# Attention stages of a hybrid encoder in another order on VectorE, GpSimd and TensorE

## The chip, the cores and the metric

The kernel runs on one core of one Trainium2 chip. The metric is the device time of one execution in microseconds; a kernel is measured by the median of several executions. The engines are named as the profile names them: PE is TensorE, DVE is VectorE, ACT is ScalarE, POOL is GpSimd, SP is SyncE (it issues the DMAs here).

## The reference, cut to what matters

Two requests, one of 1024 tokens and one of 512, go through the same two layers: a dilated sliding-window attention and a bidirectional S5 state-space layer. The change is in the attention layer and in the parameter tables of the S5 layer, which are computed beside it.

```python
def dilated_mixer(h, w_in, w_out):                       # 16 heads of 64
    proj = h @ w_in
    z = proj[..., 3 * N_DIL * ATTN_WIDTH:]
    for g, (window, dil) in enumerate(((128, 1), (512, 4), (2048, 16))):
        qkv = ...                                        # this group's 3 x 1024 columns of proj
        q = apply_rope(qkv[:, :, 0], cos, sin) * HEAD_DIM ** -0.5
        k = apply_rope(qkv[:, :, 1], cos, sin)
        o, lse = dilated_window_attention(q, k, qkv[:, :, 2], dil, window // (2 * dil))
    weights = jax.nn.softmax(jnp.stack(lses, axis=0), axis=0)
    o = jnp.einsum('gbsh,gbshe->bshe', weights, jnp.stack(outs, axis=0))
    return (o.reshape(bsz, s, ATTN_WIDTH) * jax.nn.silu(z)) @ w_out

def s5_mixer(h, ...):                                    # per direction
    lam_bar = jnp.exp(lam * dt)                          # its powers and products with B and C:
    b_bar = ((lam_bar - 1.0) / lam)[..., None] * b_mat   # the tables of the text below
    ...
```

## The kernel before, in words

The 1536 tokens are 12 tiles of 128. The attention works through units: a pair of heads p (8 of them) with one of the three dilation groups g. First come all (p, 0), then for each pair (p, 1), (p, 2) and a gate unit (p, 3). A unit with g below 3 has 12 steps, one per tile T; the gate unit has 3. A step is one projection of a tile into its q, k and v columns: 24 matmuls on PE (`gemm`, L885, 128x384 each; every product is made from a high and a low part, three matmuls for each of 8 slices).

**What sets the order.** The program is written by a small table of hooks. A step has 25 slots; before the matmul of slot m, whatever is hung at (step, m) is issued. All engines take their instructions in the order in which they are issued, and each waits, in that order, for what its next instruction needs. So the slots set the order on every engine and no time. A tile's further stages are hung at slots counted from the start of its own projection: one of 36 falls at slot 11 of the step after it, so that up to five tiles are in flight. The tables are `at` (L715) for the first part of a stage and `LATER` (L84) for its later parts, counted from the first.

```python
LATER = {"rope": (4, 7, 0), "qk": (3, 5, 3, 5), "soft": (5,), "et": (2, 4), "pv": (6, 6)}
at = {"rope": (0, 24), "qk": ... divmod(36, 25), "scores": divmod(max(76, ...), 25),
      "soft": divmod(79, 25), "et": divmod(100, 25), "pv": divmod(111, 25)}
```

A tile passes these stages, with the lines that the trace names:

- rope: DVE makes two products with the rotary table from the projection's result (L914, L915), POOL adds them up (L898, L899, tile t), ACT takes the values out (L941) and DVE their low part (L894).
- qk: PE transposes the rotated queries and keys into the PSUM tile qkT (L950, L951); ACT copies queries (L963) and keys (L965) out, and the keys a second time into the other half of the partitions (L971); DVE makes the low parts of the queries (L968) and of the keys (L974). Each of these is two instructions of 64x128, one for each head.
- scores: PE multiplies (L995, L999, tile sc).
- soft: DVE adds the mask and takes the row's extreme (L1022 in one form, L1025 twice), ACT makes the exponential (L1010).
- et: PE transposes the weights (L1043), ACT copies them (L1053, tile et), DVE makes their low part (L1055).
- pv: PE multiplies by the values (L1068); ACT copies the result out (L1077, L1078), POOL adds two parts onto the sum u or U (L1082).

Between them further work is hung:

- Conversion of the next unit's weights (`w_cvt`): eight per unit, ACT L842 and then L843, on DVE for even numbers and on POOL for odd ones; the first three stand at slot 16 of the unit's third, fifth and seventh step, the others in and behind its last step.
- The S5 tables: sixteen batches. A batch has 12 POOL operations of 128x512 (`prep_tab`, L1253 to L1260), two in each of six steps, and seven pairs of DVE operations (`prep_phase`, three operations for part 0, L1344 to L1346, and three for part 1, L1348 to L1350) in seven steps. Its tiles are zs and f.
- The combination of the previous pair's three groups (`combine`), in eight steps after each (p, 2), on DVE and POOL (L1169, L1179, L1178).

Of the kernel before, what the change touches and what calls it, by code (L numbers as in the profile page):

```python
# [10 lines left out]
F32 = mybir.dt.float32  # L11
# [3 lines left out]
AF = mybir.ActivationFunctionType  # L15
ALU = mybir.AluOpType
# [66 lines left out]

LATER = {"rope": (4, 7, 0), "qk": (3, 5, 3, 5), "soft": (5,), "et": (2, 4), "pv": (6, 6)}  # L84

# [55 lines left out]
class Kern:  # L141
# [550 lines left out]
    def attention(self):  # L692
        nc, I, tl = self.nc, self.I, self.tl
        H = tl.hook
# [8 lines left out]
        for u, (p, g) in enumerate(units):  # L703
            first = at_unit[p, g] = len(tl.items)
            n = NT if g < 3 else 3
            for T in range(n):
                if u == 0 and T < 2:
                    tl.idle(1)
                    i = T
                else:  # L710
                    i = tl.add(self.gemm, (p, g, T))
                if g < 3:
                    end = u + 2 == len(units)
                    early = u == 0 and T == 0
                    at = {"rope": (0, 24), "qk": (2, 2) if early else divmod(36, 25), "scores": divmod(max(76, 36 + 26 + max(LATER["qk"])), 25), "soft": divmod(79, 25), "et": divmod(100, 25), "pv": divmod(111, 25)}  # L715
                    if end:
# [9 lines left out]
                    if T == NT - 1:  # L726
                        st = divmod(25 * at["soft"][0] + at["soft"][1] + LATER["soft"][0], 25)
                        H(i + st[0], st[1], self.stats_out, p, g)
                        if g == 0:
                            H(i + at["pv"][0], at["pv"][1] + LATER["pv"][1] + 1, self.u0_store, p)  # L730
                        if end:
# [213 lines left out]
    def stage_qk(self, p, g, T, part=0):  # L945
        nc, A, B = self.nc, self.pools.get("A"), self.pools.get("B")
        if part == 0:
# [4 lines left out]
            return  # L952
        tp = self.state[(p, g, T, "tp")]
        if part == 1:
# [6 lines left out]
        if part == 1:  # L961
            for h, r, o in hs:
                nc.scalar.activation(qT[r, h], tp[r, 0:128], AF.Copy, scale=-0.125)  # L963
            for h, r, o in hs:
                nc.scalar.activation(kT[r, 0, h, c], tp[r, 128:256], AF.Copy)  # L965
        elif part == 2:
            for h, r, o in hs:
                nc.vector.scalar_tensor_tensor(qT[o, h], tp[r, 0:128], -0.125, qT[r, h].bitcast(F32), op0=ALU.mult, op1=ALU.subtract)  # L968
        elif part == 3:
            for h, r, o in hs:  # L970
                nc.scalar.activation(kT[o, 0, h, c], tp[r, 128:256], AF.Copy)  # L971
        else:
            for h, r, o in hs:
                nc.vector.tensor_tensor(kT[r, 1, h, c], tp[r, 128:256], kT[r, 0, h, c].bitcast(F32), op=ALU.subtract)  # L974
            self.state.pop((p, g, T, "tp"))

    def stage_scores(self, p, g, T):
# [255 lines left out]
    def prep_tab(self, which, part):  # L1233
# [18 lines left out]
        if part == 0:  # L1252
            g_.tensor_tensor(tr, x(xr), lr, op=ALU.mult)  # L1253
            g_.tensor_tensor(tt, x(xi), li, op=ALU.mult)
        elif part == 1:
            g_.tensor_tensor(tr, tr, tt, op=ALU.add if which == 0 else ALU.subtract)
            g_.tensor_tensor(ti, x(xi), lr, op=ALU.mult)
        else:
            g_.tensor_tensor(tt, x(xr), li, op=ALU.mult)
            g_.tensor_tensor(ti, ti, tt, op=ALU.subtract if which == 0 else ALU.add)  # L1260

# [97 lines left out]
    def prep_hooks(self, b, i):  # L1359

        H = self.tl.hook
        H(i, 0, self.prep_load, b)
        H(i + 1, 11, self.prep_cb, b)
        for k in range(3):
            H(i + 2 + k, 3, self.prep_tab, 0, k)
        H(i + 5, 11, self.prep_c_out, b)
        H(i + 5, 11, self.prep_lag, b, 0)
        H(i + 5, 16, self.prep_lag, b, 1)
        H(i + 5, 21, self.prep_lag_out, b, 0)
        H(i + 5, 21, self.prep_lag_out, b, 1)  # L1370
        for k in range(3):
            H(i + 6 + k, 7, self.prep_tab, 1, k)
        H(i + 9, 0, self.prep_b_out, b, 0)
        H(i + 9, 20, self.prep_b_out, b, 1)
        for j in range(7):
            H(i + 2 + j, 15, self.prep_phase, b, j, 0)
            H(i + 2 + j, 21, self.prep_phase, b, j, 1)

# [643 lines left out]
```

## Time and profile before

| what | value |
|---|---|
| runs (device us) | 3187.55, 3179.74, 3178.81; median 3179.74 |
| the profiled execution's own time | 3181.66 us |
| its span | 3179.8 us |
| granted clock of PE, mean | 0.975 of full speed |
| busy: PE, DVE, ACT, POOL | 2829.9 (89%), 2200.0 (69%), 1848.4 (58%), 1498.9 (47%) us |
| attention, units and hooks as above | about 57 to 2277 us of the span |

Busy time is what an engine spends in its instructions; the rest is idle time, and the trace names for each idle stretch the instruction whose end released the engine. Matmuls overlap in the engine, so a start of the next is a better mark than the end of the one before. A stretch (a window) of the span is given as start:end in us.

### The profile page before, as it was taken

To read this page: it belongs to the slowest core of one execution; us is meant where nothing else is said; L and a number is where in the kernel's file an instruction comes from. 1 tells how busy PE (TensorE), PEld (TensorE's weight loads), DVE (VectorE), ACT (ScalarE), POOL (GpSimd) and SP (SyncE) were. 2 spreads that over 40 slices of the span, in tenths; PEclk is the share of its full clock that TensorE was granted. 3 is DMA by queue.
4 is the path that set the end of the run, shared out by engine and by line. 5 is a ranking of instruction groups with operands and counts; after the bars stand their busy time and mean duration, and the time that the engine had idled before them with its cause. 6 is when DMAs were issued, how large, how long until landed. Compare 5 with 4: busy or idle time off the path is not lost.

```text
span 3179.8 us, 51898 instructions
## 1 busy us (share of the span) xinstructions
PE 2829.9 (89%) x16181; PEld 2439.5 (77%) x16181; DVE 2200.0 (69%) x6071; ACT 1848.4 (58%) x5696; POOL 1498.9 (47%) x2081
## 2 busy tenths in 40 slices
PE   6799999997788888888888888888989989889998
PEld 5788888887777878778787878778778766667887
DVE  7677777775776676757666676757664699984445
ACT  5877777777676766667576676667644222223221
POOL 3645555453653453535344453535365466552243
PEclk8999999998899999999999999999999999999999
DMA  7122232221122212221222222121354545436553
GB/s 205 51 85 76 83 81 77 71 85 48 45 82 56 62 48 57 57 66 44 60 58 55 58 51 66 42 72 52 96 163 123 170 158 176 164 121 182 166 159 126
DMA packets 428227, 293.73 MB, mean 92 GB/s; under 512 B 140288, under 2 KB 379152, under 8 KB 427824
## 3 DMA queue, kind: packets, MB, share of 16 engines
q1 hardware_dynamic: 427808, 290.16, 31.8%
q8 instruction: 128, 2.10, 0.3%
q14 instruction: 147, 1.20, 0.1%
q10 hardware_dynamic: 144, 0.26, 0.0%
HBM read 204.72 MB, written 85.62 MB: 91 GB/s over the span
## 4 chain that ended last, share of the span: by engine, by line
PE 38%; DVE 21%; ACT 15%; POOL 9%; issue 9%; DMA 7%; SPq 1%; POOLq 0%; DVEq 0%; ACTq 0%
PE mm L885 13%; PE mm L1652 8%; DMA wraw<-in_attn_w_in 3%; ACT e L1010 3%; ACT kT L971 2%; DVE et L1055 2%; DVE kT L974 2%; ACT kT L965 2%; PE sc L1845 2%; ACT pw L1077 2%; PE mm L1845 2%; PE pv L1068 2%; DVE t L914 2%; DVE qT L968 2%; ACT qT L963 2%
## 5 line engine op out<-in xcount | busy, mean ns | idle before, releaser
L885 PE MATMUL mm<-whl,hp 128*128 128x384 f32 x4584 | 967.3, 354 | 7.6 <-ACT hp L356 2.8
L885 PEld LDWEIGHTS mm<-whl,hp 128*128 128x128 f32 x4584 | 817.4, 197 | 27.5 <-issue 12.9
L885 PE MATMUL mm<-whl,hs 128*128 128x384 f32 x2304 | 486.5, 352 | 0.8 <-ACT hs L270 0.4
L1082 POOL TENSOR_TENSOR u<-u,pw 128x128 f32<-128x128 f32 x384 | 197.8, 515 | 523.7 <-ACT u L1078 508.1
L885 PEld LDWEIGHTS mm<-whl,hs 128*128 128x128 f32 x2304 | 406.3, 194 | 9.5 <-issue 7.2
L968 DVE SCALAR_TENSOR_TENSOR qT<-qkT,qT 64x128 fp32r<-64x128 f32 x576 | 166.4, 289 | 341.9 <-ACT kT L971 324.0
L1010 ACT ACTIVATE e<-e,st 128x128 f32<-128x128 f32 (+2 forms) x576 | 250.3, 435 | 152.1 <-DVE st L1025 151.7
L1652 PE MATMUL mm<-hp,wi 128*128 128x512 f32 x1104 | 280.8, 403 | 2.7 <-ACT sig L1689 2.7
L1068 PE MATMUL pv<-et,vs 128*128 128x256 f32 x704 | 159.2, 306 | 131.3 <-DVE et L1055 130.9
L1068 PEld LDWEIGHTS pv<-et,vs 128*128 128x128 f32 x704 | 115.3, 191 | 178.2 <-DVE et L1055 175.0
L1652 PEld LDWEIGHTS mm<-hp,wi 128*128 128x128 f32 x1104 | 203.9, 189 | 54.1 <-issue 8.6
L898 POOL TENSOR_TENSOR t<-t,t 128x128 f32<-128x128 f32 x288 | 137.7, 478 | 206.9 <-DVE t L915 195.0
L1077 ACT ACTIVATE pw<-pv 64x256 f32<-64x256 f32 x576 | 217.9, 378 | 9.8
L941 ACT ACTIVATE vs<-mm 64x128 fp32r<-64x128 f32 (+1 forms) x350 | 96.0, 274 | 206.8 <-DVE t L915 203.8
L1082 POOL TENSOR_TENSOR U<-U,pw 128x128 f32<-128x128 f32 x192 | 91.7, 478 | 238.4 <-ACT U L1078 230.9
L1055 DVE TENSOR_TENSOR et<-eT,et 128x512 fp32r<-128x512 f32 (+1 forms) x288 | 162.9, 566 | 34.7 <-ACT et L1053 34.3
L963 ACT ACTIVATE qT<-qkT 64x128 fp32r<-64x128 f32 x576 | 155.2, 269 | 54.3 <-PE qkT L951 48.0
L843 POOL TENSOR_TENSOR whl<-wraw,whl 128x384 fp32r<-128x384 f32 (+1 forms) x116 | 116.6, 1005 | 142.8 <-ACT whl L842 139.6
L974 DVE TENSOR_TENSOR kT<-qkT,kT 64x128 fp32r<-64x128 f32 x576 | 166.4, 289 | 9.8
L971 ACT ACTIVATE kT<-qkT 64x128 fp32r<-64x128 f32 x576 | 156.9, 272 | 8.1
L965 ACT ACTIVATE kT<-qkT 64x128 fp32r<-64x128 f32 x576 | 156.9, 272 | 6.8
L999 PE MATMUL sc<-kT,qT 128*128 128x192 f32 (+2 forms) x704 | 125.9, 291 | 39.1 <-DVE kT L974 38.3
(368 smaller groups left out, 6314.5 us busy)
## 6 DMA issues: line engine op xcount, KB each, us to landing
wraw<-in_attn_w_in SPq DMA_DIRECT2D x192, 192.0 KB
par<-par_d SPq DMA_DIRECT2D x64, 512.0 KB
f<-f_d SPq DMA_DIRECT2D x44, 384.0 KB
par_d<-zs SPq DMA_DIRECT2D x64, 256.0 KB
U<-in_ada_w SPq DMA_DIRECT2D x16, 768.0 KB
par_d<-f SPq DMA_DIRECT2D x64, 128.0 KB
raw<-in_ssm_w_in SPq DMA_DIRECT2D x14, 512.0 KB
u_d<-u SPq DMA_DIRECT2D x8, 768.0 KB
```

The source lines that it names most:

```text
L885: nc.tensor.matmul(ps[:, :384], self.hv(a, k, self.tok_cols(g, T)), self.wt[((p, g), k)][:, b], start=m == 0, stop=m == 23)
L963: nc.scalar.activation(qT[r, h], tp[r, 0:128], AF.Copy, scale=-0.125)
L965: nc.scalar.activation(kT[r, 0, h, c], tp[r, 128:256], AF.Copy)
L968: nc.vector.scalar_tensor_tensor(qT[o, h], tp[r, 0:128], -0.125, qT[r, h].bitcast(F32), op0=ALU.mult, op1=ALU.subtract)
L971: nc.scalar.activation(kT[o, 0, h, c], tp[r, 128:256], AF.Copy)
L974: nc.vector.tensor_tensor(kT[r, 1, h, c], tp[r, 128:256], kT[r, 0, h, c].bitcast(F32), op=ALU.subtract)
L1010: nc.scalar.activation(e[:, h, :W], e[:, h, :W], AF.Exp, scale=-1.0, bias=st[:, T, h, 0:1], accum_out=st[:, T, h, 1:2])
L1055: nc.vector.tensor_tensor(et[:, 1, 0:n], tp[:, 0:n], et[:, 0, 0:n].bitcast(F32), op=ALU.subtract)
L1068: nc.tensor.matmul(pv[:, h], V[key][:, 2 * h:2 * h + 2].rearrange("p a c -> p (a c)"), et[:, :, ci, h], start=ci == 0, stop=ci == len(chun ...
L1077: nc.scalar.activation(w[hi], pv[hi, h], AF.Copy)
L1082: nc.gpsimd.tensor_tensor(u, u, w[:, a], op=ALU.add)
L1652: nc.tensor.matmul(st["ps"], state[("w", u)][a][:, k], self.hv(b, k, slice(512 * c, 512 * c + 512)), start=m == 0, stop=m == 23)
```

## The change

Five edits, all in the order of issue but one:

1. The second copy of the keys (into the other half of the partitions) is made by POOL from the first copy in SBUF, not by ACT from PSUM. The first copy, the queries' and the keys' low parts are then hung together.
2. DVE's mask for one tile now comes ahead of the low part of the weights of the tile before, and the low part of the values moves to one slot later.
3. The queries' and keys' transposes move two matmuls later (36 to 38), the product with the values seven (111 to 118).
4. The tables on POOL are hung one operation at a time, at slots 8 and 19, instead of two at slot 3 or 7. The two additions of each half go over the tile as it lies (128x512 in one run) instead of through the four-dimensional view that the products need.
5. DVE's phase work moves from slots 15 and 21 to 18 and 22.

```diff
-LATER = {"rope": (4, 7, 0), "qk": (3, 5, 3, 5), "soft": (5,), "et": (2, 4), "pv": (6, 6)}
+LATER = {"rope": (4, 8, 0), "qk": (3, 5, 5), "soft": (5,), "et": (2, 6), "pv": (6, 6)}
...
-"qk": ... divmod(36, 25), "scores": divmod(max(76, 36 + 26 + max(LATER["qk"])), 25), ... "pv": divmod(111, 25)}
+"qk": ... divmod(38, 25), "scores": divmod(76, 25), ... "pv": divmod(118, 25)}
...
         elif part == 2:
             for h, r, o in hs:
                 nc.vector.scalar_tensor_tensor(qT[o, h], tp[r, 0:128], -0.125, ...)
-        elif part == 3:
-            for h, r, o in hs:
-                nc.scalar.activation(kT[o, 0, h, c], tp[r, 128:256], AF.Copy)
-        else:
             for h, r, o in hs:
                 nc.vector.tensor_tensor(kT[r, 1, h, c], tp[r, 128:256], kT[r, 0, h, c].bitcast(F32), op=ALU.subtract)
             self.state.pop((p, g, T, "tp"))
+        else:
+            for h, r, o in hs:
+                nc.gpsimd.tensor_copy(kT[o, 0, h, c], kT[r, 0, h, c].bitcast(F32))
...
-            g_.tensor_tensor(tr, tr, tt, op=ALU.add if which == 0 else ALU.subtract)
+            g_.tensor_tensor(P["tr"], P["tr"], P["tt"], op=ALU.add if which == 0 else ALU.subtract)
...
-            g_.tensor_tensor(ti, ti, tt, op=ALU.subtract if which == 0 else ALU.add)
+            g_.tensor_tensor(P["ti"], P["ti"], P["tt"], op=ALU.subtract if which == 0 else ALU.add)
...
-        for k in range(3):
-            H(i + 2 + k, 3, self.prep_tab, 0, k)
+        for k in range(6):
+            H(i + 2 + k // 2, (8, 19)[k % 2], self.prep_tab, 0, k)
...
-        for k in range(3):
-            H(i + 6 + k, 7, self.prep_tab, 1, k)
+        for k in range(6):
+            H(i + 6 + k // 2, (8, 19)[k % 2], self.prep_tab, 1, k)
...
-            H(i + 2 + j, 15, self.prep_phase, b, j, 0)
-            H(i + 2 + j, 21, self.prep_phase, b, j, 1)
+            H(i + 2 + j, 18, self.prep_phase, b, j, 0)
+            H(i + 2 + j, 22, self.prep_phase, b, j, 1)
```

**PE, one plain step.** The rows around the products with the values (pv, from the weights et and the values vs, ve) and the transposes of queries and keys (qkT). Before:

```order
L885 MATMUL mm<-whl,hp_122 128x384 x2
L1068 MATMUL pv<-et,vs 128x256
L1068 MATMUL pv<-et,ve_588 128x256
L1068 MATMUL pv<-et,vs 128x256
L1068 MATMUL pv<-et,ve_588 128x256
L950 MATMUL qkT<-ident,t_10951 128x128
L951 MATMUL qkT<-ident,t_10951 128x128
L885 MATMUL mm<-whl,hp_123 128x384
```

And with the change:

```order
L885 MATMUL mm<-whl,hp_531 128x384
L950 MATMUL qkT<-ident,t_10951 128x128
L951 MATMUL qkT<-ident,t_10951 128x128
L885 MATMUL mm<-whl,hp_531 128x384
L885 MATMUL mm<-whl,hp_532 128x384
L885 MATMUL mm<-whl,hp_531 128x384 x2
L885 MATMUL mm<-whl,hp_532 128x384
L1067 MATMUL pv<-et,vs 128x256
```

Before, the four products with the values stand after the projection's tenth matmul behind the scores and right ahead of the transposes; now the transposes stand after the twelfth and the products five matmuls behind them.

**DVE, a step with phase work.** From the low part of the values (L894) to the work on the next tile's rope; st is the row's extreme that the mask step leaves. Before:

```order
L1055 TENSOR_TENSOR et<-eT,et 128x2x128
L1022 TENSOR_TENSOR e<-sc,masks 128x2x128
...
L894 TENSOR_TENSOR vs<-mm,vs 128x128
L1344 TENSOR_TENSOR f<-f,p_pb 128x4x32
L1345 TENSOR_TENSOR f<-f,p_pb 128x4x32
L1346 TENSOR_TENSOR f<-f 128x4x32
L968 SCALAR_TENSOR_TENSOR qT<-qkT,qT 64x128 x2
L974 TENSOR_TENSOR kT<-qkT,kT 64x128 x2
L1348 TENSOR_TENSOR f<-f,p_pb 128x4x32
```

With the change (lines of the new file: L970 is the keys' low part, L1346 to L1352 the phase work, L1021 and L1024 the mask, L1054 the weights' low part):

```order
L968 SCALAR_TENSOR_TENSOR qT<-qkT,qT 64x128 x2
L970 TENSOR_TENSOR kT<-qkT,kT 64x128 x2
L1346 TENSOR_TENSOR f<-f,p_pb 128x4x32
L1347 TENSOR_TENSOR f<-f,p_pb 128x4x32
...
L1352 TENSOR_TENSOR f<-f 128x4x32
L914 TENSOR_TENSOR t_14352<-mm,rope 128x256
L915 TENSOR_TENSOR t_14353<-mm,rope 128x256
L1021 TENSOR_TENSOR e<-sc,masks 128x2x128
...
L1054 TENSOR_TENSOR et<-eT,et 128x2x128
```

The first three phase operations moved from ahead of the queries' and keys' low parts to behind them, and the weights' low part from ahead of the mask to behind it.

**POOL, the same step.** From the additions of one tile's rope (L898, L899) to those of the next. Before:

```order
L899 TENSOR_TENSOR t_16471<-t_16471,t_16472 128x4x32
L1256 TENSOR_TENSOR zs<-zs 128x4x8x16
L1257 TENSOR_TENSOR zs<-p_bb,p_pb 128x4x8x16
L1082 TENSOR_TENSOR U_1800<-U_1800,pw 128x128 x2
L898 TENSOR_TENSOR t_16552<-t_16552,t_16553 128x4x32
```

With the change (L974 is now POOL's copy of the keys):

```order
L899 TENSOR_TENSOR t_16471<-t_16471,t_16472 128x4x32
L1256 TENSOR_TENSOR zs<-zs 128x512
L974 CAST kT<-kT 64x128 x2
L1258 TENSOR_TENSOR zs<-p_bb,p_pb 128x4x8x16
L1081 TENSOR_TENSOR U_1800<-U_1800,pw 128x128 x2
L898 TENSOR_TENSOR t_16552<-t_16552,t_16553 128x4x32
```

One of the two table operations now stands behind the keys' copies and ahead of the additions to the sum and of the next rope's.

## Rows read from the trace of the kernel before

**Rows 1.** Stretches: us; busy (instructions) PE, PEld, DVE, ACT, POOL; PEclk; DMA; GB/s

```profile
57.00:822.00 765.00, 675.19 (x4277) 605.61 (x4277) 569.46 (x1797) 584.37 (x1802) 386.57 (x564) 0.96 0.25 71
1023.00:2277.00 1254.00, 1101.01 (x6538) 996.60 (x6536) 861.54 (x2762) 844.10 (x2907) 561.32 (x884) 0.98 0.22 56
```

**Rows 2.** Waits of PE, 57 to 822 us: in total, times, longest

```profile
PE pv L1068 <- DVE et L1055: 40.7, 33, 5.9
PE sc L999 <- DVE kT L974: 31.8, 29, 4.4
```

**Rows 3.** The same waits of PE, 1023 to 2277 us

```profile
PE pv L1068 <- DVE et L1055: 95.5, 95, 2.2
PE qkT L950 <- POOL t L899: 43.3, 88, 1.7
```

**Rows 4.** Timeline of one plain step: start, duration, engine, line, tiles [idle before]

```profile
900.15 0.27 PE L950 MATMUL qkT<-ident,t 128*128 128x128 f32 x1
...
900.29 2.51 PE L885 MATMUL mm<-whl,hs 128*128 128x384 f32 x13
...
900.57 0.56 ACT L963 ACTIVATE qT<-qkT 64x128 fp32r<-64x128 f32 x2 [1.03 <-PE qkT L951]
...
901.71 0.56 ACT L971 ACTIVATE kT<-qkT 64x128 fp32r<-64x128 f32 x2
...
902.29 0.59 DVE L968 SCALAR_TENSOR_TENSOR qT<-qkT,qT 64x128 fp32r<-64x128 f32 x2 [3.37 <-ACT kT L971]
...
904.29 0.69 DVE L1055 TENSOR_TENSOR et<-eT,et 128x512 fp32r<-128x512 f32 x1
...
905.23 0.28 PE L1068 MATMUL pv<-et,vs 128*128 128x256 f32 x1
...
905.70 0.27 PE L950 MATMUL qkT<-ident,t 128*128 128x128 f32 x1
```

**Rows 5.** Stretches of the third pair, chosen by kind of step (columns as rows 1)

```profile
1210.34:1265.23 54.89, 48.57 (x296) 44.96 (x297) 40.78 (x116) 37.10 (x125) 24.11 (x35) 1.00 0.21 55
1270.89:1286.06 15.17, 11.72 (x66) 10.08 (x64) 8.38 (x33) 10.20 (x36) 6.79 (x11) 1.00 0.39 102
1291.69:1311.90 20.21, 16.72 (x98) 15.07 (x96) 16.25 (x56) 13.39 (x50) 14.87 (x23) 1.00 0.09 23
1319.64:1341.66 22.02, 17.11 (x102) 15.45 (x100) 21.21 (x56) 13.52 (x48) 13.51 (x18) 1.00 0.11 26
```

**Rows 6.** Timeline of a step with table work on GpSimd and VectorE

```profile
1325.84 2.07 POOL L1256 TENSOR_TENSOR zs<-zs 128x512 f32<-128x512 f32 x1
...
1327.83 1.26 POOL L1257 TENSOR_TENSOR zs<-p_bb,p_pb 128x512 f32<-128x512 f32 x1
...
1327.97 1.20 DVE L1345 TENSOR_TENSOR f<-f,p_pb 128x128 f32<-128x128 f32 x1
...
1330.13 0.59 DVE L974 TENSOR_TENSOR kT<-qkT,kT 64x128 fp32r<-64x128 f32 x2
1330.73 0.29 DVE L1348 TENSOR_TENSOR f<-f,p_pb 128x128 f32<-128x128 f32 x1
```

**Rows 7.** Timeline of the step at a unit's last tile

```profile
1275.85 0.56 DVE L843 TENSOR_TENSOR whl<-wraw,whl 128x384 fp32r<-128x384 f32 x1 [1.14 <-ACT whl L842]
...
1277.58 0.50 PE L1068 MATMUL pv<-et,vs 128*128 128x256 f32 x2 [1.60 <-DVE et L1055]
...
1281.52 0.63 PE L885 MATMUL mm<-whl,hp 128*128 128x384 f32 x2 [0.63 <-POOL whl L843]
```

**Rows 8.** Timeline of a step with the previous pair's combination

```profile
1258.62 0.33 PE L950 MATMUL qkT<-ident,t 128*128 128x128 f32 x1 [1.70 <-POOL t L899]
```

**Rows 9.** GpSimd's lines by form: busy us, mean ns, idle before

```profile
L898 POOL TENSOR_TENSOR t<-t,t 128x128 f32<-128x128 f32 x288 | 137.7, 478 | 206.9 <-DVE t L915 195.0 <-PE sc L999 6.5 <-DVE hs L813 1.9
...
L810 POOL COPY U<-hs 128x512 f32<-128x512 f32 x16 | 17.7, 1133 | 0.0
```

**Rows 10.** VectorE's lines by form: the smallest shapes of the phase work

```profile
L1349 DVE TENSOR_TENSOR f<-f,p_pb 128x8 f32<-128x8 f32 x16 | 2.8, 175 | 0.0
```

More of the change, by code (lines that the diff above doesn't have):

```diff
@@ L714, in attention @@
                     early = u == 0 and T == 0
-                    at = {"rope": (0, 24), "qk": (2, 2) if early else divmod(36, 25), "scores": divmod(max(76, 36 + 26 + max(LATER["qk"])), 25), "soft": divmod(79, 25), "et": divmod(100, 25), "pv": divmod(111, 25)}
+                    at = {"rope": (0, 24), "qk": (2, 2) if early else divmod(38, 25), "scores": divmod(76, 25), "soft": divmod(79, 25), "et": divmod(100, 25), "pv": divmod(118, 25)}
                     if end:
@@ L729, in attention @@
                         if g == 0:
-                            H(i + at["pv"][0], at["pv"][1] + LATER["pv"][1] + 1, self.u0_store, p)
+                            H(i + at["pv"][0] + (at["pv"][1] + LATER["pv"][1] + 1) // 25, (at["pv"][1] + LATER["pv"][1] + 1) % 25, self.u0_store, p)
                         if end:
@@ L952, in stage_qk @@
             return
-        tp = self.state[(p, g, T, "tp")]
+        tp = self.state.get((p, g, T, "tp"))
         if part == 1:
@@ L1253, in prep_tab @@
             g_.tensor_tensor(tr, x(xr), lr, op=ALU.mult)
+        elif part == 1:
             g_.tensor_tensor(tt, x(xi), li, op=ALU.mult)
-        elif part == 1:
-            g_.tensor_tensor(tr, tr, tt, op=ALU.add if which == 0 else ALU.subtract)
+        elif part == 2:
+            g_.tensor_tensor(P["tr"], P["tr"], P["tt"], op=ALU.add if which == 0 else ALU.subtract)
+        elif part == 3:
             g_.tensor_tensor(ti, x(xi), lr, op=ALU.mult)
-        else:
-            g_.tensor_tensor(tt, x(xr), li, op=ALU.mult)
-            g_.tensor_tensor(ti, ti, tt, op=ALU.subtract if which == 0 else ALU.add)
+        elif part == 4:
+            g_.tensor_tensor(tt, x(xr), li, op=ALU.mult)
+        else:
+            g_.tensor_tensor(P["ti"], P["ti"], P["tt"], op=ALU.subtract if which == 0 else ALU.add)
     def prep_c_out(self, b):
```

## The prediction, made before the change was run

> **What bounds the kernel now.** I read the stretches first [rows 1]. From 57 to 822 us (the (p, 0) units) PE is busy 675.19 of 765 us, from 1023 to 2277 us (the (p, 1), (p, 2) and gate units) 1101.01 of 1254 us; between them lie some steps that regroup the tokens. So 90 and 153 us are idle, and only they can be won: the change takes nothing off PE. Then PE's waits by line [rows 2, 3]. In the first stretch 40.7 us go to the products with the values, which wait for the weights' low part on DVE, and 31.8 us to the scores, which wait for the keys' low part. In the second 95.5 us go to the values' products and 43.3 us to the transposes, which wait for rope's additions on POOL. These waits are the ceiling: 72.5 and 138.8 us, 211 us in all.
>
> The plain step [rows 4] shows why a small disturbance becomes a wait. Transposes at 900.15; ACT's six copies from 900.57 to 902.27; then DVE in a row: queries' and keys' low parts, from 902.29, two rope products, the weights' low part from 904.29 to 904.98; PE's values' products at 905.23 and the next transposes at 905.70. The loop from transposes to transposes goes once round in 5.55 us, which is also what PE's own work fills (13 matmuls in 2.51 us, 0.193 each). There is no slack: whatever DVE or POOL do besides is waited for.
>
> **The change, step by step.** Times are against the profiled execution, 3181.66 us (span 3179.8); it stands 1.9 us above the median 3179.74, so I carry the difference over to the median.
>
> The new loop. DVE may start when ACT has made four copies, not six: 0.57 us earlier. The weights' low part leaves the loop, since the values' products no longer stand ahead of the transposes. What remains is 0.42 to ACT, 1.13 for four copies, 1.23 for the two low parts, 0.77 for rope's products, 1.1 for POOL's additions (two of 0.478 [rows 9] and the hand-overs): 4.7 us. PE needs 5.55, so the plain step has 0.85 us to spare where it had none.
>
> The values' products come 7 x 0.193 = 1.35 us later. Against this the mask now stands ahead of their low part; it lies beside the matmuls. Likewise the scores: the keys' low part is ready 0.57 us earlier, at the same slot. What is new in their way is POOL's copy, 64x128, twice. Lower bound: 128/512 of the 1.133 us copy, 0.28; upper: an addition of the same length with two inputs, 0.478 [rows 9]. I take 0.36, nearer to the copy because it has one input: 0.72 us for two, beside DVE's 1.23, hidden as long as POOL is free at that moment.
>
> Does POOL's copy hold up the low parts beside it? In the table step [rows 6] DVE's L1345, with both inputs in SBUF, takes 1.20 us while POOL's L1257 runs, and ends when that ends; the like L1348 alone takes 0.29. But L974, with one input in PSUM, takes its usual 0.59 for two. So the low parts go on and the phase work is held. The Trainium skill, "SBUF — State Buffer", section "Who interferes with whom", says the same: a VectorE instruction with two SBUF inputs contends with a GpSimd one that reads SBUF, and the second to come is fully blocked. By that rule the weight conversion on DVE is exposed too.
>
> Now the kinds of step, in the third pair [rows 5]:
>
> - *Eight steps with combination work*, 54.89 us, 6.3 idle; the wait is the transposes' for rope's additions, up to 1.70 [rows 8], behind a POOL addition. New: 4.7 + one 1.26 POOL operation [rows 6] = 6.0, in steps where DVE too stands behind one 7.2; mean 6.6, eight give 52.8: **-2.1**. Bounds 0 and -6.3.
> - *The last tile and the step after it*, 15.17 us, 3.45 idle: 1.60 before the values' products, behind a conversion of 0.56 on DVE, and 0.63 on a late weight [rows 7]. 1.35 later plus the shorter ACT part covers the first; I keep 0.3: **-3.1**. Bounds 0 and -3.45.
> - *Table steps j0 to j2*, 20.21 us. All six phase operations now lie in the loop, between the keys' low part and rope: 6 x 0.175 [rows 10] = 1.05, plus a block B by POOL. B: the second table operation starts when the copies are done, 0.72 after DVE began its low parts, and lasts 1.26, so it ends 0.75 after DVE reaches the phase work; I take 0.9. Bounds: 0, if it is over by then; 1.7, if both 0.48 additions to the sum follow it in turn. Three steps of 4.7 + 1.05 + 0.9, and a conversion on DVE with a short block (0.86), which at slot 16 now stands ahead of the low parts: 20.86, **+0.65**.
> - *Table steps j4 to j6*, 22.02 us. Operations of 0.22 (estimate between the two rows), 0.29 and 0.42 (estimate by width), six each, 5.6; three times 4.7 + 0.9; a conversion with a block, 1.1: 23.5, **+1.5**. In both kinds POOL gains: the strided addition of 2.07 should take the 1.26 of its contiguous neighbour.
> - *The rest*, 1 us idle: **-0.9**.
>
> That is -3.95 a pair; the stretch is 7.3 pairs long (1254 us by steps of some 6.4, 27 to a pair): **-29**.
>
> In the (p, 0) units half of the scores' 31.8 us goes (-16): the waits of a few tenths go, those up to 4.4 us are not made by the order. Of the values' 40.7 us I let a quarter go (-10). Conversions ahead of the low parts cost 0.56 to 1 us in some 14 steps (+11), phase work 3: **-12**.
>
> Sum -41 us: 3140.7 for a profiled execution, **3139 us** for the median.
>
> **The rivals.**
>
> *Nearly all waits go.* If blocks are short (B near 0.2) and the combination steps fit the PE's own time, the table steps gain 0.7 us each: 96 steps (16 batches of six), 67 us, capped by the waits left; some 50 more than forecast: 3087 us. For it: DVE is idle a quarter of the second stretch [rows 1]. Against it: the table steps alone have DVE busy 21.21 of 22.02 [rows 5], and their work stays.
>
> *The lock makes it slower.* Before, the first phase operations stood outside the tight part, and ran while ACT copied. Now all six come in a row at the moment at which POOL has the table operation and then two additions to the sum queued, all reading SBUF. If each POOL operation gets its turn between two of DVE's, as L1257 did behind L1256 [rows 6], B is 1.7 to 1.8, not 0.9: a step loses 0.8, 96 steps 67 to 70, the sum turns to +27: 3206 us. It decides from B = 1.33 on (41/96 above 0.9). For it: those two rows. Against it: the additions to the sum wait for ACT's copies of products that come five matmuls behind the transposes, so they may come too late to interlock. The rule of the Trainium skill named above is the one that speaks against this change: GpSimd's copies and single table operations at slot 19 put more SBUF reads beside two-input VectorE work.
>
> *Nothing moves.* POOL is 561 us busy of 1254 [rows 1] and gets 576 copies of 0.36, 207 us. If they queue behind table and combination work, the scores wait for them as the values' products did before: what is won at one line comes back at another, 3178 us. The same result follows if DVE is released as late as before, by a later event on ACT than the fourth copy.
>
> **How the numbers follow.** Forecast (3105 to 3168) 0.46, nearly all waits go 0.22, nothing moves 0.13, the lock 0.19. A measurement can tell about 0.3%, 9.5 us, from no change. Faster by more: 0.46 + 0.22 = 0.68; within: 0.13; slower: 0.19. The range leaves out the far part of the first rival (below 3085, 0.08) and of the lock (above 3194, 0.11); it takes in the bounds of the terms (-15 and +6 for the combination, +-0.5 in B on half the steps). Likeliest case alone: 3105 to 3168.
>
> **What would show it.** Right: the values' products' 95.5 us fall below 40; DVE's L968 starts within 0.05 us of the end of the fourth copy; POOL's copies near 0.36; last-tile steps near 6.0; POOL's table additions near 1.26; table steps unchanged or a little longer with the transposes' wait for POOL as what is left. The lock: phase operations L1346 to L1352 at 0.8 us and more and the transposes' wait well above 43.3 us. Nothing moves: the scores' wait rises in place of the values'. The prediction is wrong in kind if PE's busy time changes, or if the gain lies outside 57 to 2277 us.

## The result, and the profile after

The changed kernel took 3138.95 us (median of 4 runs, 3135.5 to 3140.71), the kernel before, run beside it, 3182.09 us (median of 4 with the runs shown above). The ratio is 0.9861, 95% interval 0.9843 to 0.988: faster by 43 us, 1.4%. The forecast was 3139 us. The number was right, in part by luck: the loop that the change shortens is there, but of the terms for the kinds of step two promised 3.6 us a pair of heads too much and two 2.8 us too little, and these nearly cancelled.

The profiled execution of the changed kernel has a span of 3138.9 us. First its stretches, by the same boundaries in the program (columns as in [rows 1] and [rows 5]):

```profile
57.00:807.00 750.00, 664.41 (x4280) 595.78 (x4281) 552.69 (x1794) 531.80 (x1613) 421.15 (x756) 0.96 0.26 73
1005.00:2235.00 1230.00, 1075.04 (x6529) 989.84 (x6529) 815.06 (x2761) 759.22 (x2560) 637.15 (x1216) 0.98 0.23 57
1190.05:1244.47 54.42, 47.01 (x293) 44.05 (x292) 40.61 (x115) 33.34 (x111) 29.33 (x51) 1.00 0.21 56
1250.09:1264.90 14.81, 12.67 (x69) 11.96 (x68) 9.08 (x32) 9.48 (x33) 7.28 (x15) 0.88 0.48 126
1270.00:1289.68 19.68, 17.41 (x129) 15.74 (x129) 14.06 (x60) 12.55 (x46) 14.93 (x29) 1.00 0.14 40
1296.76:1318.60 21.84, 16.39 (x100) 15.35 (x100) 16.60 (x57) 11.91 (x41) 14.49 (x24) 1.00 0.07 15
```

From 57 to 807 us stands what took 57 to 822 before [rows 1], to within a microsecond or two: 750 us against 765. The second stretch takes 1230 us against 1254, the regrouping between them (807 to 1005) 198 against 201, and all behind it 904 against 903. So the gain lies where it was expected: 15, 3 and 24 us. But PE's idle time in the second stretch is 1230 - 1075 = 155 us, and was 153 [rows 1]. The gain does not show as less idle time at all; PE's busy time fell, by 26 us, with the same 6500 matmuls. A matmul that waits shortly is counted as busy until the modelled end of the one before. Measured from start to start, less the idle time printed, the middle value from a projection matmul to a PE instruction of another kind behind it is 0.34 us where there is a wait and 0.18 where there is none, in both kernels. So a wait of up to 0.16 us is not seen as idle. Before, such waits stood in two places of a step: ahead of the values' products (0.28 us from the projection matmul in the mean of the second stretch, now 0.18) and between these products and the transposes (0.21 us, where 0.12 is usual without a wait). The length of a step tells more than the idle time in it, if the same instructions are compared.

PE's waits, first of the stretch from 57 to 807 us, then of 1005 to 2235 us:

```profile
PE qkT L950 <- POOL t L899: 46.6, 46, 3.2
PE sc L998 <- DVE kT L970: 17.0, 16, 3.3
PE sc L998 <- POOL kT L974: 13.5, 13, 4.2
PE pv L1067 <- DVE et L1054: 3.8, 3, 2.0
```

```profile
PE qkT L950 <- POOL t L899: 117.1, 89, 2.8
...
PE pv L1067 <- DVE et L1054: 10.6, 7, 2.9
```

The values' products waited 40.7 and 95.5 us before [rows 2, 3]; now 3.8 and 10.6. The transposes' wait for rope's additions on POOL rose from 43.3 to 117.1 us in the second stretch, and in the first to 46.6, from 2.9. One place of waiting took over from the other: PE now stops once in a step, at the end of the loop.

The step of [rows 4], the tenth of the first pair's (p, 1) unit, in the timeline of the changed kernel:

```profile
884.16 0.27 PE L950 MATMUL qkT<-ident,t 128*128 128x128 f32 x1
...
885.14 0.57 ACT L965 ACTIVATE kT<-qkT 64x128 fp32r<-64x128 f32 x2
...
885.54 0.63 POOL L974 CAST kT<-kT 64x128 fp32r<-64x128 f32 x2 [2.42 <-ACT kT L965]
...
885.74 0.59 DVE L968 SCALAR_TENSOR_TENSOR qT<-qkT,qT 64x128 fp32r<-64x128 f32 x2 [3.05 <-ACT kT L965]
...
887.51 1.00 POOL L1081 TENSOR_TENSOR u<-u,pw 128x128 f32<-128x128 f32 x2 [1.34 <-ACT u L1077]
...
888.47 0.45 POOL L898 TENSOR_TENSOR t<-t,t 128x128 f32<-128x128 f32 x1
...
889.72 0.27 PE L950 MATMUL qkT<-ident,t 128*128 128x128 f32 x1
```

DVE starts its low parts at 885.74, 0.03 us behind ACT's fourth copy (885.14 and 0.57); POOL's copies, 0.63 for two, are done before DVE's second low part begins at 886.34. The next transposes follow at 5.57 us, with no wait; before it was 5.55. Steps of a (p, 2) unit have two products with the values and two transposes of the weights where this one has four of each, and take 5.1 us when PE does not wait.

A table step (the one that answers to [rows 6]):

```profile
1303.62 1.28 POOL L1256 TENSOR_TENSOR zs<-zs 128x512 f32<-128x512 f32 x1
...
1303.72 0.33 PE L950 MATMUL qkT<-ident,t 128*128 128x128 f32 x1 [1.65 <-POOL t L899]
...
1305.88 1.21 POOL L1258 TENSOR_TENSOR zs<-p_bb,p_pb 128x512 f32<-128x512 f32 x1
...
1306.57 0.57 DVE L1346 TENSOR_TENSOR f<-f,p_pb 128x128 f32<-128x128 f32 x1
...
1307.07 0.55 DVE L1347 TENSOR_TENSOR f<-f,p_pb 128x128 f32<-128x128 f32 x1
...
1310.72 0.33 PE L950 MATMUL qkT<-ident,t 128*128 128x128 f32 x1 [1.69 <-POOL t L899]
```

POOL's addition L1256 takes 1.28 us where it took 2.07. The phase operations L1346 to L1348 take 0.57, 0.55 and 0.50 beside POOL's L1258 and the additions that follow it, where 0.29 would be their own time [rows 6]: held, but shortly. The transposes at 1310.72 come 7.00 us behind those at 1303.72, and wait 1.69 us of it.

### The profile page after: what moved, and what is told of

It is laid out like the page before. It is cut to its first block, busy times and chain, and to the rows that moved or that the text cites. A ratio compares the mean times of both kernels' runs of the same rounds, so it can differ in the third digit from the quotient of the medians.

```text
span 3138.9 us, 52520 instructions
## 1 busy us (share of the span) xinstructions
PE 2788.1 (89%) x16181; PEld 2419.8 (77%) x16181; DVE 2131.3 (68%) x6071; ACT 1700.8 (54%) x5120; POOL 1620.9 (52%) x2657
## 5 line engine op out<-in xcount | busy, mean ns | idle before, releaser
L885 PE MATMUL mm<-whl,hp 128*128 128x384 f32 x4584 | 992.0, 353 | 5.1 <-ACT hp L356 2.8
L885 PEld LDWEIGHTS mm<-whl,hp 128*128 128x128 f32 x4584 | 804.1, 196 | 22.2 <-issue 12.0
L885 PE MATMUL mm<-whl,hs 128*128 128x384 f32 x2304 | 498.6, 350 | 0.0
L885 PEld LDWEIGHTS mm<-whl,hs 128*128 128x128 f32 x2304 | 398.1, 192 | 7.5 <-issue 7.2
L968 DVE SCALAR_TENSOR_TENSOR qT<-qkT,qT 64x128 fp32r<-64x128 f32 x576 | 166.4, 289 | 304.1 <-ACT kT L965 297.9
L974 POOL CAST kT<-kT 64x128 fp32r<-64x128 f32 x576 | 171.2, 297 | 316.9 <-ACT kT L965 297.3
L1009 ACT ACTIVATE e<-e,st 128x128 f32<-128x128 f32 (+2 forms) x576 | 249.3, 434 | 52.4 <-DVE st L1024 48.4
L1081 POOL TENSOR_TENSOR u<-u,pw 128x128 f32<-128x128 f32 x384 | 188.7, 491 | 167.8 <-ACT u L1077 152.1
L950 PE MATMUL qkT<-ident,t 128*128 128x128 f32 x288 | 89.5, 311 | 184.4 <-POOL t L899 182.3
L1076 ACT ACTIVATE pw<-pv 64x256 f32<-64x256 f32 x576 | 217.5, 378 | 36.2 <-PE pv L1067 25.5
L898 POOL TENSOR_TENSOR t<-t,t 128x128 f32<-128x128 f32 x288 | 137.8, 478 | 187.2 <-DVE t L915 180.2
L950 PEld LDWEIGHTS qkT<-ident,t 128*128 128x128 f32 x288 | 40.7, 141 | 241.5 <-POOL t L899 238.5
L843 POOL TENSOR_TENSOR whl<-wraw,whl 128x384 fp32r<-128x384 f32 (+1 forms) x116 | 113.8, 981 | 139.9 <-ACT whl L842 138.5
L843 DVE TENSOR_TENSOR whl<-wraw,whl 128x384 fp32r<-128x384 f32 (+1 forms) x108 | 85.0, 787 | 138.5 <-ACT whl L842 138.0
L970 DVE TENSOR_TENSOR kT<-qkT,kT 64x128 fp32r<-64x128 f32 x576 | 166.3, 289 | 9.8
L1054 DVE TENSOR_TENSOR et<-eT,et 128x512 fp32r<-128x512 f32 (+1 forms) x288 | 163.5, 568 | 6.6 <-ACT et L1052 6.3
L1081 POOL TENSOR_TENSOR U<-U,pw 128x128 f32<-128x128 f32 x192 | 90.7, 472 | 147.6 <-ACT U L1077 140.1
L1067 PE MATMUL pv<-et,vs 128*128 128x256 f32 x704 | 147.8, 290 | 19.6 <-DVE et L1054 17.6
```

Source lines behind the costliest of these rows:

```text
L843: (nc.gpsimd if start or k in (1, 3, 5, 7) else nc.vector).tensor_tensor(w[:, 1], raw, w[:, 0].bitcast(F32), op=ALU.subtract)
L885: nc.tensor.matmul(ps[:, :384], self.hv(a, k, self.tok_cols(g, T)), self.wt[((p, g), k)][:, b], start=m == 0, stop=m == 23)
L974: nc.gpsimd.tensor_copy(kT[o, 0, h, c], kT[r, 0, h, c].bitcast(F32))
L1009: nc.scalar.activation(e[:, h, :W], e[:, h, :W], AF.Exp, scale=-1.0, bias=st[:, T, h, 0:1], accum_out=st[:, T, h, 1:2])
L1054: nc.vector.tensor_tensor(et[:, 1, 0:n], tp[:, 0:n], et[:, 0, 0:n].bitcast(F32), op=ALU.subtract)
L1067: nc.tensor.matmul(pv[:, h], V[key][:, 2 * h:2 * h + 2].rearrange("p a c -> p (a c)"), et[:, :, ci, h], start=ci == 0, stop=ci == len(chun ...
```

## The experiments

Differences below are of medians, against 3139 us; the runs of the kernel before that stand beside them had medians of 3180 to 3184 us, so a difference is good to some 3 us.

| run | what is different from the changed kernel | median us | ratio to before, 95% interval |
|---|---|---|---|
| changed | - | 3139 | 0.9861 (0.9843 to 0.988) |
| keys_act_early | edit 1 undone | 3187 | 1.0009 (0.9997 to 1.002) |
| keys_act_late | ACT copies the keys again, later | 3274 | 1.028 (1.0257 to 1.0302) |
| pv_111_low_first | edit 2 (but for the values' low part) and the product's part of edit 3 undone | 3382 | 1.0636 (1.059 to 1.0681) |
| pv_111_adds_behind | the same, POOL's queue set right | 3207 | 1.0078 (1.0063 to 1.0093) |
| low_first | edit 2 alone undone, as far as above | 3166 | 0.9962 (0.9947 to 0.9977) |
| strided | edit 4's additions undone | 3167 | 0.9959 (0.9942 to 0.9975) |
| tab_pairs | edit 4's hooks undone | 3113 | 0.9788 (0.977 to 0.9806) |
| phase_15_21 | edit 5 undone | 3080 | 0.9669 (0.9654 to 0.9683) |
| cvt_9 | two conversions on DVE moved | 3100 | 0.9744 (0.9726 to 0.9762) |
| phase15_cvt9 | both of these | 3041 | 0.9558 (0.9542 to 0.9574) |
| phase15_cvt9_tab_pairs | and the table in pairs | 3083 | 0.9702 (0.968 to 0.9725) |
| phase15_cvt9_comb | the best, combination moved | 3050 | 0.9595 (0.9573 to 0.9617) |

**The keys' second copy.** It goes back to ACT, behind the first (`keys_act_early`) or where POOL's stands (`keys_act_late`):

```diff
-LATER = {... "qk": (3, 5, 5), ...}
+LATER = {... "qk": (3, 5, 3), ...}          # keys_act_early alone
-                nc.gpsimd.tensor_copy(kT[o, 0, h, c], kT[r, 0, h, c].bitcast(F32))
+                nc.scalar.activation(kT[o, 0, h, c], tp[r, 128:256], AF.Copy)
```

> The changed kernel (3139 us) with the keys' second copy on ACT again, right behind the first, so that DVE starts its low parts after six copies, not four. Theory A (the gain is the shorter loop: DVE is released 0.57 us earlier, and the transposes wait for that loop in 149 steps): each of these steps is 0.57 us longer, up to +85 us, 3190 to 3224 us, with the transposes' wait for POOL well above 182 us. Theory B (the gain is that PE stops once in a step instead of twice, because the values' products no longer wait): the stops stay at one a step, +0 to +25 us.

Measured: 3186.75 us, +48. Timeline of a step (L973 is the second copy):

```profile
1257.56 0.56 ACT L973 ACTIVATE kT<-qkT 64x128 fp32r<-64x128 f32 x2
...
1258.15 0.59 DVE L968 SCALAR_TENSOR_TENSOR qT<-qkT,qT 64x128 fp32r<-64x128 f32 x2 [2.47 <-ACT kT L973]
```

DVE's low parts start behind the sixth copy, 0.57 us later. The transposes' wait for POOL rises from 182.3 to 205.9 us over the whole run. This edit alone is worth about the whole net gain, and theory A, the length of the loop, stands; the lower end of its range was missed by 3 us. Theory B by itself gave at most +25, and falls.

> The changed kernel with the keys' second copy on ACT, but hung where POOL's copy hangs, behind the hook of DVE's low parts: DVE is released after four copies, POOL has 576 copies of 0.297 us (171 us) less. Theory A: as the changed kernel or a little better, 3120 to 3140 us, since the loop is the same and POOL is freer. Theory B: the same. A rival, that POOL's copies gave something that ACT can't (ACT's copies of the values' results come 0.57 us later): 3140 to 3165 us. If DVE is held until the sixth copy all the same, as in the kernel before, the run is like the one with the early copy.

Measured: 3273.51 us, +135; both theories missed it. Timeline of a plain step:

```profile
1397.41 0.56 ACT L973 ACTIVATE kT<-qkT 64x128 fp32r<-64x128 f32 x2 [1.26 <-DVE kT L970]
...
1399.43 1.00 POOL L1080 TENSOR_TENSOR U<-U,pw 128x128 f32<-128x128 f32 x2 [4.93 <-ACT U L1076]
...
1401.30 0.33 PE L950 MATMUL qkT<-ident,t 128*128 128x128 f32 x1 [1.42 <-POOL t L899]
```

ACT's late copy waits 1.26 us until DVE's low part L970 is done, and all that ACT has queued behind it waits too: the copies of the values' result (L1076), so POOL's additions to the sum (L1080 in this file), so rope's additions behind them, so the transposes, 1.42 us. The plain step takes 6.75 us. ACT's copy does not use what L970 writes; in the trace it waits on the semaphore that L970 raises, so the program itself holds this wait. The same is seen in the kernel before and in `keys_act_early`, where DVE's L968 was released by the keys' second copy on ACT ([rows 4], and the fence above), whose result it does not use. In all three one engine's reads of qkT waited for the reads that were issued to the other engine before; POOL's copy reads SBUF and is free of it. Why the program has these waits stays open. Shown is that a wait in the middle of ACT's queue goes round the loop.

**The values' products.** Back to 111, with the weights' low part first:

```diff
-"pv": divmod(118, 25)     -"et": (2, 6)
+"pv": divmod(111, 25)     +"et": (2, 4)
```

> The changed kernel with the values' products back seven matmuls earlier (111) and the weights' low part ahead of the mask again; the rest as changed. Theory A (shorter loop): about the gain stays, 3139 to 3150 us. Theory B (one stop of PE instead of two): the values' products wait again in 100 steps and more, each stop 0.2 to 0.3 us beside the idle time in the profile, 3160 to 3180 us.

Measured: 3381.69 us, +243, far outside both. PE's waits over the whole run, and a step of the timeline:

```profile
PE sc L998 <- POOL kT L974: 164.7, 103, 5.6
PE pv L1067 <- DVE et L1054: 161.1, 110, 6.3
```

```profile
1351.00 1.00 POOL L843 TENSOR_TENSOR whl<-wraw,whl 128x384 fp32r<-128x384 f32 x1 [2.73 <-ACT whl L842]
...
1352.37 0.99 POOL L1081 TENSOR_TENSOR u<-u,pw 128x128 f32<-128x128 f32 x2 [0.37 <-ACT u L1077]
...
1353.43 0.64 POOL L974 CAST kT<-kT 64x128 fp32r<-64x128 f32 x2
1353.77 0.65 PEld L998 LDWEIGHTS sc<-kT,qT 128*128 128x128 f32 x4 [2.31 <-POOL kT L974]
```

With the products at 111 POOL's additions to the sum (L1081) are hung at slot 17, and so stand ahead of the keys' copies at slot 18. The copies' input is there at 1350.37 and POOL's conversion (L843) is done at 1352.00, but L1081 waits for ACT's results and the copies run at 1353.43; the scores wait 2.06 us. Such waits make 164.7 us in 103 stops. So edit 1 needs edit 3: the later product is what keeps POOL's queue in the right order. The next run has the products at 111 too, and only POOL's additions two slots later:

```diff
-"pv": (6, 6)
+"pv": (6, 8)
```

> As the run with the values' products at 111 (3382 us), but POOL's additions to the sum hung two slots later, so that they stand behind the keys' copies in POOL's queue and not ahead of them. Theory Q (that run was slow because the keys' copies stood behind additions that wait for ACT, 164.7 us of the scores' waits in 103 stops): 3160 to 3210 us, and what is left over 3139 us is the price of the earlier products and of the low part ahead of the mask. Rival (the values' products' 161 us of waits are what costs): 3320 us and more.

Measured: 3207.08 us, +68. Theory Q holds: 175 of the 243 us were the queue. Of the 68 the next run tells the part of the order on DVE, with the products at 118:

```diff
-"et": (2, 6)
+"et": (2, 4)
```

> The changed kernel with the weights' low part ahead of the mask again, the values' products staying at 118. Neither is in the loop from transposes to transposes, so by the loop theory nothing changes, 3132 to 3146 us. If the order of the two matters of itself (the exponential and all behind it come 0.4 to 0.7 us later), the values' products wait for the weights again: 3150 to 3180 us.

Measured: 3166.35 us, +27, as the alternative had it, but by another way than it gave: the values' products do not wait more. ACT's wait ahead of the exponential, in the changed kernel and then in this one:

```profile
ACT e L1009 <- DVE st L1024: 48.4, 99, 3.2
```

```profile
ACT e L1009 <- DVE st L1024: 156.5, 244, 3.8
```

With the low part first the mask is late, ACT waits for it ahead of the exponential (156.5 us instead of 48.4), and the exponential stands in ACT's queue ahead of the copies of queries and keys. In the third step of the fourth pair's (p, 2) unit, a table step, these copies start 0.80 us behind the transposes instead of 0.49, and the step takes 6.44 us instead of 6.13; the plain steps are as long as before. The mask's place is in the loop after all, in the table steps, through ACT's queue.

**The table work.**

```diff
-            H(i + 2 + k // 2, (8, 19)[k % 2], self.prep_tab, 0, k)      # tab_pairs; the second half at 7
+            H(i + 2 + k // 2, 3, self.prep_tab, 0, k)
...
-            g_.tensor_tensor(P["tr"], P["tr"], P["tt"], ...)            # strided; the same for ti
+            g_.tensor_tensor(tr, tr, tt, ...)
```

> The changed kernel with the table operations on POOL two at a time at slots 3 and 7 again, the additions left in one run. If hanging them singly is what makes room (the second stands behind the keys' copies instead of ahead of them): the copies start 0.9 us later in 96 steps and the scores or the transposes wait, 3150 to 3190 us. If the second at slot 19 costs (it holds DVE's phase work and stands ahead of rope's additions): 3105 to 3135 us.

> The changed kernel with the table additions through the four-dimensional view again (2.07 us each instead of 1.30, 64 of them). Half stand at slot 8, ahead of the keys' copies, half at slot 19, ahead of rope's additions. If POOL's time at these places is in the loop: 32 by 0.8 and a part of the other 32, 3160 to 3185 us. If it is covered: 3139 to 3148 us.

Measured: 3113.2 us, -26, and 3167.03 us, +28. The second table operation at slot 19 costs, and the contiguous additions gain; edit 4 comes out even.

**The phase work and the conversions.**

```diff
-            H(i + 2 + j, 18, self.prep_phase, b, j, 0)                  # phase_15_21
-            H(i + 2 + j, 22, self.prep_phase, b, j, 1)
+            H(i + 2 + j, 15, self.prep_phase, b, j, 0)
+            H(i + 2 + j, 21, self.prep_phase, b, j, 1)
...
-[(first + 2, 16), (first + 4, 16), (first + 6, 16), ...]                # cvt_9
+[(first + 2, 9), (first + 4, 16), (first + 6, 9), ...]
```

> The changed kernel with DVE's phase work at slots 15 and 21 again, the first part ahead of the queries' and keys' low parts. If the phase work in the tight part of the loop is what costs in the table steps, its first part (0.5 to 1.3 us a step) leaves the loop: 112 steps by up to 0.5, 3090 to 3125 us. If it is held by POOL's operation at slot 8 and so holds the low parts: 3139 to 3170 us.

Measured: 3080.06 us, -59, more than the range had. The phase work takes longer on DVE there, 250 us in sum instead of 215, since its first part stands beside POOL's operation at slot 8 again. It costs less all the same, because that part now lies where DVE waits for ACT:

```profile
1240.70 0.79 DVE L1346 TENSOR_TENSOR f<-f,p_pb 128x16 f32<-128x16 f32 x1
...
1242.08 0.59 DVE L968 SCALAR_TENSOR_TENSOR qT<-qkT,qT 64x128 fp32r<-64x128 f32 x2 [0.29 <-ACT kT L965]
```

L1346 is held to 0.79 us, and DVE still waits 0.29 us for ACT's copies behind the three operations.

> The changed kernel with two of the next unit's weight conversions on DVE (the third and seventh step of a unit) at slot 9 instead of 16, that is ahead of ACT's copies of queries and keys, where DVE stands idle, and no longer between these and their low parts. If they are in the loop now (the second step of a (p, 1) unit takes 8.12 us, before 6.86; 0.95 from the end of ACT's copies to the low parts): 23 units by two by 0.5 to 0.9 us, 3098 to 3116 us. If the loop of these steps is set by something else (the combination, the table work): 3130 to 3140 us.

Measured: 3099.72 us, -39. A conversion in the second step of a (p, 1) unit of the changed kernel, 8.04 us long, and POOL's second addition of rope at the end of that step:

```profile
1192.19 0.56 DVE L843 TENSOR_TENSOR whl<-wraw,whl 128x384 fp32r<-128x384 f32 x1 [0.99 <-ACT whl L842]
...
1192.78 0.59 DVE L968 SCALAR_TENSOR_TENSOR qT<-qkT,qT 64x128 fp32r<-64x128 f32 x2
...
1196.50 1.54 POOL L899 TENSOR_TENSOR t<-t,t 128x128 f32<-128x128 f32 x1
1196.69 1.02 DVE L1177 TENSOR_TENSOR f<-f,U 128x512 f32<-128x512 f32 x1
...
1198.10 0.33 PE L950 MATMUL qkT<-ident,t 128*128 128x128 f32 x1 [1.59 <-POOL t L899]
```

The conversion waits for ACT's L842, then takes 0.56, and the low parts begin at 1192.78 instead of 1191.64. This is what the run takes out. It is not what makes the step longer than before (6.85 us in this pair): there the conversion stood behind the low parts, and rope's products began 4.64 us behind the transposes, here 4.69. The difference is L899, 1.54 us here. In the same step of the kernel before:

```profile
1216.69 0.45 POOL L899 TENSOR_TENSOR t<-t,t 128x128 f32<-128x128 f32 x1
...
1216.93 1.14 DVE L1178 TENSOR_TENSOR f<-f,U 128x512 f32<-128x512 f32 x1
```

L1177 (L1178 before) is the combination's product of 128x512 with both inputs in SBUF. Before, it started 0.24 us behind L899, L899 took its usual 0.45, and the product 1.14. Now it starts 0.19 us behind, takes 1.02, and L899 ends 0.32 us behind its end. It is so in all seven pairs of the stretch (L899 1.51 to 1.54 us, before 0.45 or 0.46). In the fifth step the product starts 0.15 us ahead of L899 (before 0.13 behind it), and L899 takes 1.25 us. With the conversions at slot 9 the fifth step is free of this (L899 0.46), the second is not.

> The phase work's first part at slot 15 (3080 us alone) together with the conversions at slot 9. If both are separate pieces taken out of the same loop, the gains add up: 3080 less the gain of the conversions alone, 3040 to 3060 us. If both need the same idle stretch of DVE ahead of the low parts, less than that in the steps that have both: 3060 to 3080 us.

Measured: 3041.44 us, -98: 59 and 39 add up. This is the best of all that was run, 4.4% faster than the kernel before and 3.1% than the changed one. What is left of the transposes' wait over the whole run, 182.3 us in the changed kernel:

```profile
PE qkT L950 <- POOL t L899: 121.8, 125, 3.8
```

> The kernel with phase work at slot 15 and conversions at 9 (3041 us) with POOL's table operations in pairs at slots 3 and 7 too, which alone gave 26 us. If the gains add up: 3010 to 3025 us. If the pair (2.5 us) runs beside the phase work's first part, which now stands at the same moment, it holds it up as in the kernel before, and the low parts behind it: 3045 to 3080 us.

Measured: 3082.98 us, +42 against the best: the gain of the pairs turns round. By form, the phase operations of 128x128, of the best and then of this one:

```profile
L1346 DVE TENSOR_TENSOR f<-f,p_pb 128x128 f32<-128x128 f32 x16 | 13.2, 822 | 0.0
...
L1347 DVE TENSOR_TENSOR f<-f,p_pb 128x128 f32<-128x128 f32 x16 | 4.7, 295 | 0.0
```

```profile
L1347 DVE TENSOR_TENSOR f<-f,p_pb 128x128 f32<-128x128 f32 x16 | 17.3, 1084 | 0.0
...
L1346 DVE TENSOR_TENSOR f<-f,p_pb 128x128 f32<-128x128 f32 x16 | 15.0, 940 | 0.0
```

With the phase work's first part at slot 15 a single table operation holds one of DVE's operations, a pair holds two, 1.08 and 0.94 us instead of 0.295 and 0.822, and the low parts stand behind them. This is the arrangement of the kernel before [rows 6].

> The same kernel (3041 us) with the combination's second to fourth part hung at slot 9 of the next step and slots 3 and 14 of the one after, instead of slots 22, 14 and 24: out of the stretch between the low parts and rope, with POOL's additions of 1.29 us behind rope's. If they are what is left in the loop (transposes wait 0.8 to 1.6 us in the steps that have them, 21 rounds of three steps): 3005 to 3030 us. If the load of the next part's factors, now issued later, or the later mask takes it back: 3035 to 3060 us.

```diff
-enumerate(((0, 10), (0, 22), (1, 14), (1, 24)))
+enumerate(((0, 10), (1, 9), (2, 3), (2, 14)))
```

Measured: 3050.3 us, +9. The first round gains (its first step falls from 7.42 to 5.54 us in the mean of the second to seventh pair; L899 there takes 0.46 us again), the later ones lose it:

```profile
1173.26 1.26 DVE L1164 TENSOR_TENSOR f<-f,u 128x512 f32<-128x512 f32 x1 [3.58 <-DMA f<-f_d]
...
1175.48 0.68 PE L998 MATMUL sc<-kT,qT 128*128 128x192 f32 x3 [2.69 <-DVE kT L970]
```

The next factors are loaded by the last part of the round before. That part comes later now, the load with it, and DVE waits 3.58 us for the DMA with the low parts queued behind.

## Why the prediction came out right, and where it was wrong

*The new loop* is there, but longer than it was worked out. DVE is released by the fourth copy, POOL's copies take 0.297 each (0.36 was taken), the table's additions on POOL 1.30 (1.26), and the transposes' wait for POOL is what is left. Undoing edit 1 costs 48 us. But the loop of the plain step is 5.2 us, not 4.7: in the step shown above rope's products are done at 887.79, and rope's additions start only at 888.47, behind POOL's additions to the sum (L1081, 1.00 us), which the forecast's sum of the loop leaves out. PE's 5.55 us held (5.57 now, with no wait), so the step has 0.4 us to spare and not 0.85.

*The kinds of step*, in us a pair; the mean is that of the second to seventh pair:

| kind | forecast | third pair [rows 5] | mean |
|---|---|---|---|
| combination, eight steps | -2.1 | -0.47 | -0.38 |
| last tile and the step after | -3.1 | -0.36 | -1.25 |
| table steps j0 to j2 | +0.65 | -0.53 | -0.57 |
| table steps j4 to j6 | +1.5 | -0.18 | -0.10 |
| the rest | -0.9 | +0.4 | -0.7 |
| a pair | -3.95 | -1.1 | -3.0 |

The first two lines fell short by 3.6 us in the mean, the next two were better by 2.8. That the sum came out near is luck to this extent.

*The combination steps.* The sum took a lock of VectorE and GpSimd to hold DVE only. It holds POOL too: the second and fifth step of a (p, 1) unit have rope's addition L899 held by the combination's product, 1.5 and 1.25 us instead of 0.45 (above). These 1.9 us a pair are about what is missing. The second step went from 6.86 to 8.12 us (means), most of it by this. The conversions at slot 16 stand in this loop too, as `cvt_9` shows, but they did so before. That a start 0.05 us earlier turns the order round could not be worked out beforehand from [rows 8].

*The last tile.* The values' products no longer wait there, as said. But the conversions in that step now do what they did:

```profile
1253.29 1.11 ACT L842 ACTIVATE whl<-wraw 128x384 fp32r<-128x384 f32 x2 [1.65 <-DMA wraw<-in_attn_w_in]
...
1254.43 0.94 DVE L843 TENSOR_TENSOR whl<-wraw,whl 128x384 fp32r<-128x384 f32 x1 [1.57 <-ACT whl L842]
...
1257.72 0.33 PE L950 MATMUL qkT<-ident,t 128*128 128x128 f32 x1 [2.14 <-POOL t L899]
```

ACT's L842 waits 1.65 us for a weight's DMA, DVE's conversion behind it ends at 1255.37, and rope's products start only then; the transposes wait 2.14 us. The prediction looked at the wait before the products and not at what stands between the low parts and rope. In the third pair the granted clock fell besides (0.88 in the mean of that stretch; see the last section). And some 0.46 us are only moved between this line and the rest: two small transposes of the tables (L1215, L1216 before) stood behind the queries' and keys' transposes at the start of the (p, 2) unit, and now stand ahead of them, in the step after the last tile. The first step of the (p, 2) unit, 5.62 us before and 5.12 now, is shorter by that and not by a wait; like for like the line is about -1.7 and the rest about -0.2.

*The table steps.* The block B was too large: the phase work's sum on DVE fell from 313 to 215 us, and 192 us were reached with the table in pairs, so B is at least (215 - 192)/96 = 0.24 us a step; in the step shown some 0.7, not 0.9.

*The rest* holds gains and a loss that the forecast had no term for: the gate unit's steps grew by 0.9 us a pair, where PE's wait for DVE's L1134 (L1135 before) rose from 9.4 to 15.5 us in the second stretch.

*Small slips* changed little: the terms of the steps j0 to j2 give 20.81 us and not 20.86; seven matmuls are 1.2 us from start to start and not 1.35; DVE was idle for 31% of the second stretch [rows 1], more than a quarter; and a pair took 182.6 us before, so the stretch is 6.9 pairs long and not 7.3.

*The lock rival* had the right place and too large a price. It stood at 3206 us with B = 1.7 (0.8 us in 96 steps are 77 us and not 67 to 70, so by its own terms it would be some 8 us later still). Edit 5 does cost 59 us against leaving the phase work where it was, and the lock can't be most of it, as the run with the earlier slot shows: there the same operations take 35 us more on DVE and the kernel 59 us less. What counts is that they left the loop. The rule of the Trainium skill, "SBUF — State Buffer", section "Who interferes with whom", is borne out by the run with pairs: an operation of 0.29 us with two inputs in SBUF takes 1.08 beside POOL's. What the rival left out is that DVE's work holds POOL as well.

*The sums.* (p, 0) units -15 (forecast -12), regrouping -3 (0), second stretch -24 (-29). In the (p, 0) units the parts were off too: the scores were to give 16 us and gave one (31.8 before, 17.0 + 13.5 now), the values' products were to give 10 and gave 37, and the transposes took 44 of it. One edit undone at a time, the change is worth +48 for the keys, +68 for the product's slot and the mask, +28 for the contiguous additions, and -26 and -59 for the single table operations and the phase work: 59 us if they added up, 43 measured. The prediction had no term for what each edit does by itself, so it could not see that two of the five cost 85 us.

## What to carry to other kernels

Find the loop first: follow what releases a stage round all engines until it comes back, and write down everything that stands in each engine's queue between two members of it; here POOL's additions to the sum were forgotten, 0.5 us of a loop of 5.2. An operation costs its time there and nothing in a stretch where its engine waits anyway, even if contention makes it longer. Compare steps that hold the same instructions, since a moved stage also moves what is counted into a step. A stage that is moved changes the order in every queue that it issues to: try each edit by itself, since a gain of 1.4% here held two edits that lost 2.7%.

## What was not expected of the hardware

Waits of up to 0.16 us in front of a matmul don't appear as idle time of PE in this profile: the second stretch is 24 us shorter with 2 us more of idle time.

Which of two engines is held turns on tenths of a microsecond. DVE's product of 128x512 with two inputs in SBUF and POOL's rope addition ran at the same time in both kernels. Where the product started 0.24 or 0.13 us behind the addition, the addition kept its 0.45 us and the product took 1.14 or 1.26 instead of 1.02. Where it started 0.19 us behind or 0.15 ahead, the addition ended 0.32 us after the product, after 1.5 or 1.25 us. It was so in each of the seven pairs.

The step behind the last tile's wait lasts 7.19 us in the third pair and 7.20 in the sixth, but 5.62 in four others with a wait of the same kind (2.14 to 2.79 us). Windows of the third pair's, the wait and the time behind it:

```profile
1255.60:1257.70 2.10, 0.00 (x0) 0.00 (x0) 1.93 (x9) 0.99 (x4) 1.73 (x4) 1.00 0.53 153
1257.70:1261.00 3.30, 3.28 (x13) 3.29 (x14) 1.07 (x4) 2.79 (x12) 1.58 (x3) 0.55 0.27 32
```

The granted clock was 1.00 until the wait and 0.55 in the 3.3 us behind it, next to the lower of the two levels (1.2 of 2.4 GHz). So such a wait can cost more than its length, but doesn't each time.
